# One transformer-like layer: gates closed in written order, squares one block later, and the last write of a triangular inverse moved with its transfers

## The chip, the cores and the metric

The kernel runs on one core of a Trainium2 chip. The metric is the device time of one execution in microseconds, the median of several runs. The engines of the core are TensorE (PE, matmuls), VectorE (DVE), ScalarE (ACT), GpSimd (POOL) and the DMA queues, some of them issued by SyncE (SP). Each engine runs its own list of instructions in the order in which the program holds them, and waits on semaphores for the others.

## What is computed

One layer of a hybrid decoder on 1024 tokens of width 1024, batch 1:

```python
h  = rms_norm(x)
P  = h @ W_in              # all heads and the gates
A  = rwkv7(P)              # 8 heads x 64, delta-rule state
B  = stick_breaking(P)     # 8 heads x 64, causal, QK-norm
M  = memory_attention(P)   # 4 heads x 128, 256 memory tokens, QK-norm
x += (sum_b sigmoid(G_b) * (branch_b @ W_br[b])) @ W_out
x += conv_ffn(rms_norm(x))
```

In stick-breaking attention a token's weight for an earlier token is a sigmoid times the product of one minus the sigmoids of all tokens between, a scan along the keys. The memory attention is a softmax over 256 tokens. The RWKV heads are computed in chunks of 64 tokens, and each chunk needs the inverse of a 64 x 64 triangular matrix.

## The kernel before, in words

Every product with weights runs in split precision: `split_w` (L77 to L91) loads a weight tile `wr` of 128 x 1024, ACT rounds it to `wh` (L80), POOL takes the rest `wl` (L81), and `mm3` gives PE three matmuls for one, all recorded at L115. `wh` and `wl` have two buffers each, so the L80 of the weights after next waits until PE has read the last of the present ones. A `proj_item` is one such product: 8 steps over the inner dimension, two PSUM banks `mm` as its result, and a `yield` after each step, so that it can be cut into pieces. A `gate_item` is a projection followed by an eviction (ACT, L820), a product with the norm (DVE, L821) and, as `close`, a sigmoid (ACT, L824) and a store to DRAM (`gsd`). Closes are collected in `open_gates` and run at step 4 of the next projection (`close_gates`).

The layer is written as a chain of main parts, each woven with a stream of such items (`weave`, `pumped`): after each yield of the main part a ratio says how many pieces of the stream follow. The main parts are the preparation of RWKV (up to about 325 us of the span), `sb_attn` (to about 620), `mem_attn` (with items that must come before it, to about 760), and `stage2`, the second half of RWKV; behind them come the branches, the output projection and the feed-forward part. A second filler, `inverse`, is advanced from `pumped` as well: `pace[0]` says how many tenths of a step per piece, 7 during `sb_attn` and 16 during `mem_attn`. It builds the triangular inverses in the tile `inst` with 62 pairs of DVE operations (L545 into a temporary `it`, one buffer, and L547 back into `inst`), writes the diagonal of ones (L549) and sends the result to DRAM in 16 transfers `td` (L554), issued by POOL. Stage 2 uses a tile `it` too, the next user of that one buffer, and clears it on POOL (L564).

A unit of `sb_attn` has a `front` (PE makes scores in one or two PSUM banks `g`; ACT's sigmoid L920 reads them out), `weigh` (the scan L926 on DVE), `mid` (PE transposes, L105, into banks `g`; ACT copies them out, L938) and `back` (PE; ACT L961 reads out). There are four banks `g` and four `mm`. The stream's items at this time are, for each of four pairs of heads p, the k projection, a gate, the q projection and another gate. Their `fin` functions evict with L842 and L871 and then square (L843, L872) for the norm of the heads: PE sums the squares in a bank `g`, DVE reads it (`head_norm`, L766 and L170), POOL finishes the scale (L171, then L770 or L772, tiles `hf` and `nf`). L863 to L866 split the keys and L881, L882 the queries into high and low parts.

A block of `mem_attn` has the same shape: PE makes scores in two banks `g`; DVE takes the maximum (L1137) and from it and the head's scale `hf` a bias `nb` (L1140); ACT runs the exponential (L1143) four times for a block, in place of the read-out; DVE normalises (L1147, L1149). Two blocks later PE transposes and ACT evicts (L1158), again two blocks later PE multiplies with the values, ACT evicts (L1168) and stores. There are 8 blocks, two for each head. The items woven with it are memory queries (`mem_q`, evictions L1105 to L1107) and gates.

What fixes the order: PE's matmuls are `pinned`, which keeps them in the order in which they are written; so are the inverse's two operations, the scan and L1105 and L1107. `ordered` does the same for one instruction anywhere. All other instructions of ACT, DVE, POOL and the queues are placed by the scheduler, which runs through the program with its own costs and takes what is ready by priority; what stands first in an engine's list can therefore change when anything near it changes.

## Time and profile before

| | us |
|---|---|
| median of 3 runs | 1806.98 (1806.52 to 1807.33) |
| the profiled execution | 1807.54 |
| its span, first to last instruction | 1805.8 |
| PE busy | 1779.9 |
| DVE / ACT / POOL busy | 1178.7 / 864.3 / 789.1 |
| granted TensorE clock | 0.999 |

In a line of the timeline stand: start, duration, engine, source line, operation, what it writes and reads with shapes, how many instructions the line gathers (x), and in brackets the idle time of the engine before it with what ended it. Matmuls overlap: a line of several matmuls is busy a little beyond the start of the next. Most lines are given with source lines of the kernel before; in the changed file everything below the inverse stands two or three lines later (L772 is L774 there, L920 is L923, L1158 is L1161).

### The profile page before, as it was taken

To read this page: it belongs to the slowest core of one execution; us is meant where nothing else is said; L and a number is where in the kernel's file an instruction comes from. 1 tells how busy PE (TensorE), PEld (TensorE's weight loads), DVE (VectorE), ACT (ScalarE), POOL (GpSimd) and SP (SyncE) were. 2 spreads that over 40 slices of the span, in tenths; PEclk is the share of its full clock that TensorE was granted. 3 is DMA by queue.
4 is the path that set the end of the run, shared out by engine and by line. 5 is a ranking of instruction groups with operands and counts; after the bars stand their busy time and mean duration, and the time that the engine had idled before them with its cause. 6 is when DMAs were issued, how large, how long until landed. Compare 5 with 4: busy or idle time off the path is not lost.

```text
span 1805.8 us, 27326 instructions
## 1 busy us (share of the span) xinstructions
PE 1779.9 (99%) x10479; PEld 1442.8 (80%) x10479; DVE 1178.7 (65%) x1625; ACT 864.3 (48%) x1556; POOL 789.1 (44%) x448
## 2 busy tenths in 40 slices
PE   9999999999999999999999999989999999999998
PEld 7777778888888888777777878868888888878877
DVE  5667775898987534244444872587767777794596
ACT  6444344566566535534444334544444444454343
POOL 3223353322231462122332541487677677545454
PEclk9999999999999999999999999999999999999999
DMA  5155564211112352567654552323323333395475
GB/s 208 59 163 176 196 209 156 73 42 45 53 56 88 113 131 78 191 241 267 216 187 176 185 199 106 105 88 113 109 88 107 109 111 111 119 341 191 137 261 181
DMA packets 122628, 261.29 MB, mean 145 GB/s; under 512 B 28665, under 2 KB 43385, under 8 KB 122370
## 3 DMA queue, kind: packets, MB, share of 16 engines
q1 hardware_dynamic: 84882, 193.70, 32.4%
q10 hardware_dynamic: 33840, 53.23, 8.0%
q0 software_dynamic: 3776, 12.62, 2.3%
q8 instruction: 82, 1.34, 0.3%
q14 instruction: 48, 0.39, 0.1%
HBM read 178.99 MB, written 80.48 MB: 144 GB/s over the span
## 4 chain that ended last, share of the span: by engine, by line
PE 66%; DVE 7%; issue 3%; DMA 3%; ACT 3%; POOL 2%; ACTq 0%; DVEq 0%; POOLq 0%; SPq 0%
PE mm L115 55%; PE g L115 8%; PE g L105 3%; DMA wr<-in_w_out_dram 1%; DVE at L926 1%; DVE it L545 1%; POOL wl L81 1%; DMA A<-yd 1%; DVE da L1735 1%; DVE at L1287 0%; DVE mg L1294 0%; DVE inst L547 0%; DMA dx<-x2d 0%; DMA out_dram<-dx 0%; ACT at L1143 0%
## 5 line engine op out<-in xcount | busy, mean ns | idle before, releaser
L81 POOL TENSOR_TENSOR wl<-wr,wh 128x1024 fp32r<-128x1024 f32 (+2 forms) x78 | 195.2, 2504 | 502.1 <-ACT wh L80 492.5
L115 PE MATMUL mm<-xhi,wh 128*128 128x512 f32 x784 | 259.9, 412 | 0.5 <-DVE w L322 0.4
L115 PE MATMUL mm<-xlo,wh 128*128 128x512 f32 x784 | 243.7, 392 | 0.3 <-DVE xlo L199 0.3
L115 PE MATMUL mm<-xhi,wl 128*128 128x512 f32 x784 | 242.5, 391 | 0.0
L115 PEld LDWEIGHTS mm<-xlo,wh 128*128 128x128 f32 x784 | 147.2, 188 | 34.0 <-DVE xlo L199 1.1
L115 PEld LDWEIGHTS mm<-xhi,wl 128*128 128x128 f32 x784 | 146.8, 188 | 33.0 <-POOL wl L81 0.7
L115 PEld LDWEIGHTS mm<-xhi,wh 128*128 128x128 f32 x784 | 136.6, 189 | 28.7 <-issue 6.1
L80 ACT ACTIVATE wh<-wr 128x1024 fp32r<-128x1024 f32 (+2 forms) x78 | 81.8, 1048 | 146.8 <-PE mm L115 94.5
L115 PE MATMUL mm<-dw,da 128*128 128x512 f32 x528 | 121.9, 390 | 1.5 <-DVE da L1735 1.3
L115 PE MATMUL mm<-BT,l 128*128 128x512 f32 x504 | 118.0, 389 | 1.6 <-POOL l L1465 1.6
L115 PEld LDWEIGHTS mm<-dw,da 128*128 128x128 f32 x528 | 98.7, 188 | 24.0 <-DVE da L1735 3.1
L1736 POOL TENSOR_TENSOR dw<-draw,dw 128x512 fp32r<-128x512 f32 x55 | 81.8, 1496 | 82.5 <-ACT dw L1734 82.5
L115 PEld LDWEIGHTS mm<-BT,l 128*128 128x128 f32 x504 | 94.5, 188 | 21.6 <-POOL l L1465 2.0
L926 DVE TENSOR_TENSOR_SCAN at<-at,nrt 128x128 f32<-128x128 f32 (+3 forms) x64 | 94.2, 1478 | 25.5 <-ACT at L920 25.3
L115 PE MATMUL mm<-BT,wh 128*128 128x512 f32 x352 | 108.8, 390 | 1.6 <-DVE BT L1375 0.9
L115 PE MATMUL mm<-B,wh 128*128 128x512 f32 x352 | 108.5, 389 | 0.0
L1735 DVE TENSOR_TENSOR da<-draw,da 128x512 fp32r<-128x512 f32 x77 | 65.7, 863 | 58.7 <-ACT da L1733 58.2
L115 PE MATMUL g<-dw,da 128*128 128x512 f32 x396 | 90.8, 390 | 2.1 <-POOL dw L1736 1.1
L1465 POOL TENSOR_TENSOR l<-it,l 128x1024 fp32r<-128x1024 f32 x21 | 50.8, 2417 | 92.2 <-ACT l L1462 92.2
L115 PEld LDWEIGHTS g<-dw,da 128*128 128x128 f32 x396 | 74.3, 188 | 18.2 <-POOL dw L1736 1.4
L821 DVE TENSOR_TENSOR w<-w,nrt 128x1024 f32<-128x1024 f32 x24 | 49.8, 2076 | 58.5 <-ACT w L820 47.6
L1733 ACT ACTIVATE da<-draw 128x512 fp32r<-128x512 f32 x77 | 48.3, 628 | 82.6 <-PE mm L115 38.7
(335 smaller groups left out, 3977.9 us busy)
## 6 DMA issues: line engine op xcount, KB each, us to landing
wr<-in_w_in_dram SPq DMA_DIRECT2D x48, 512.0 KB, 3.6
draw<-actd SPq DMA_DIRECT2D x77, 256.0 KB, 4.0
draw<-in_w_down_dram SPq DMA_DIRECT2D x55, 256.0 KB, 4.9
at<-scr SPq DMA_DIRECT2D x24, 512.0 KB, 5.9
wr<-in_w_up_dram SPq DMA_DIRECT2D x22, 512.0 KB, 3.5
actd<-gall ACTq DMA_DIRECT2D x44, 256.0 KB, 3.5
rw<-in_w_up_dram SPq DMA_DIRECT2D x20, 512.0 KB, 3.7
gsd<-w ACTq DMA_DIRECT2D x18, 512.0 KB, 2.8
```

The lines of the kernel that those rows point to most:

```text
L80: self.nc.scalar.activation(hi, raw, AF.Copy)
L81: self.nc.gpsimd.tensor_tensor(lo, raw, hi.bitcast(F32), ALU.subtract)
L105: self.pinned(self.nc.tensor.transpose(out, in_, self.ident[:n, :n]))
L115: self.pinned(self.nc.tensor.matmul(*a, **k))
L545: self.pinned(nc.vector.tensor_tensor(tv, X[:, 0:s, s : s + 1].to_broadcast([128, s, n]), X[:, s : s + 1, s + 1 : 64].to_broadcast([128, s ...
L821: nc.vector.tensor_tensor(g, g, self.nrb, ALU.mult)
L926: self.pinned(nc.vector.tensor_tensor_scan(sn[:, :W][:, ::-1], sn[:, :W][:, ::-1], self.nrt[:, 1152 - W :][:, ::-1], 1.0, ALU.mult, ALU.max))
L1465: nc.gpsimd.tensor_tensor(lo, src, hi.bitcast(F32), ALU.subtract)
L1733: self.pinned(nc.scalar.activation(A[:, 0], a, AF.Copy))
L1735: self.pinned(nc.vector.tensor_tensor(A[:, 1], a, A[:, 0].bitcast(F32), ALU.subtract))
L1736: nc.gpsimd.tensor_tensor(Wt[:, 1], w, Wt[:, 0].bitcast(F32), ALU.subtract)
```

## The change

Five edits. (1) The inverse pauses for 8 more steps before it writes the diagonal, and that write keeps its written place; the inverse's steps during `mem_attn` come at half the rate (8 in place of 16), which spreads its 16 transfers. (2) The sigmoid that closes a gate keeps its written order on ACT. (3) The k projection of the first attention closes gates at its step 6, all others at 4 as before. (4) The squares of k and q are taken out of the read-out functions and run as hooks of the gate behind each: k's at step 1, q's at step 0. (5) The low half of the memory queries (L1107) is no longer pinned.

```diff
--- before.py
+++ after.py
@@ -546,7 +546,9 @@
             yield
             self.pinned(nc.vector.tensor_tensor(X[:, 0:s, s + 1 : 64], X[:, 0:s, s + 1 : 64], tv, ALU.add))
             yield
-        nc.vector.memset(X.rearrange("p s t -> p (s t)")[:, 0 : 64 * 64 : 65], 1.0)
+        for _ in range(8):
+            yield
+        self.ordered(nc.vector.memset(X.rearrange("p s t -> p (s t)")[:, 0 : 64 * 64 : 65], 1.0))
         for p in range(4):
             for h2 in range(2):
                 for cc in range(2):
@@ -772,14 +774,14 @@
         nc.gpsimd.tensor_tensor(v3(f), v3(f), b3(self.rsc), ALU.mult)
         return f
 
-    def proj_item(self, src, fin, hook={}):
+    def proj_item(self, src, fin, hook={}, close=4):
         w = self.split_w(src)
         yield
         out = [self.ps("mm"), self.ps("mm")]
         for k in range(8):
             ks = slice(k * 128, (k + 1) * 128)
             self.mm3(out, [a[:, ks] for a in w], self.xin(k), k == 0, k == 7)
-            if k == 4:
+            if k == close:
                 self.close_gates()
             if k in hook:
                 hook[k]()
@@ -821,7 +823,7 @@
             nc.vector.tensor_tensor(g, g, self.nrb, ALU.mult)
 
             def close():
-                nc.scalar.activation(g, g, AF.Sigmoid, scale=-1.0)
+                self.ordered(nc.scalar.activation(g, g, AF.Sigmoid, scale=-1.0))
                 if keep is None:
                     nc.scalar.dma_start(self.gsd[b, d], g)
                 else:
@@ -840,7 +842,6 @@
             kr, sq = self.t4(), self.t4()
             for h in range(2):
                 nc.scalar.activation(kr[:, h * 512 : (h + 1) * 512], pp[h], AF.Copy)
-            nc.scalar.activation(sq, kr, AF.Square)
             st["k"] = sq, kr
 
         def k_ss():
@@ -869,8 +870,10 @@
             qr, sq = self.t4(), self.t4()
             for h in range(2):
                 nc.scalar.activation(qr[:, h * 512 : (h + 1) * 512], pp[h], AF.Copy)
-            nc.scalar.activation(sq, qr, AF.Square)
             st["q"] = sq, qr
+
+        def square(name):
+            nc.scalar.activation(*st[name], AF.Square)
 
         def q_split(i):
             qr = st["q"][1]
@@ -888,9 +891,9 @@
             st["f"] = self.head_norm(self.head_ss(st["q"][0]), 2, SBD, SBD ** -0.5, nf)
 
         w = self.I["w_in"]
-        hooks = {1: lambda: k_split(1), 3: q_ss, 4: lambda: q_split(0), 6: lambda: q_split(1)}
+        hooks = {0: lambda: square("q"), 1: lambda: k_split(1), 3: q_ss, 4: lambda: q_split(0), 6: lambda: q_split(1)}
         kq = {4: k_bc, 5: lambda: k_split(0)}
-        return self.proj_item(w[18 + p], k_fin), k_ss, self.proj_item(w[14 + p], q_fin, kq), hooks
+        return self.proj_item(w[18 + p], k_fin, close=6), k_ss, self.proj_item(w[14 + p], q_fin, kq), {1: lambda: square("k")}, hooks
 
     def sb_attn(self, qk, need):
         nc = self.nc
@@ -1104,7 +1107,7 @@
                 hs = slice(i * 512, (i + 1) * 512)
                 self.pinned(nc.scalar.activation(qhi[:, hs], pp[i], AF.Copy, scale=self.par("memq")))
                 nc.scalar.activation(sq[:, hs], pp[i], AF.Square)
-                self.pinned(nc.vector.scalar_tensor_tensor(qlo[:, hs], pp[i], self.par("memq"), qhi[:, hs].bitcast(F32), ALU.mult, ALU.subtract))
+                nc.vector.scalar_tensor_tensor(qlo[:, hs], pp[i], self.par("memq"), qhi[:, hs].bitcast(F32), ALU.mult, ALU.subtract)
             st.extend((sq, qhi, qlo))
 
         def ss():
@@ -1868,8 +1871,8 @@
         gate = lambda hook={}: self.gate_item(*gq.pop(0), hook)
         mark = lambda name: lambda: marks.add(name)
         for p in range(4):
-            kp, kss, qp, hooks = self.sb_qk(p, qk[p])
-            items += [*([self.differ] if p == 0 else []), kp, gate({6: self.spread_last} if p == 0 else {}), kss, qp, gate(hooks), mark(f"sb{p}")]
+            kp, kss, qp, early, hooks = self.sb_qk(p, qk[p])
+            items += [*([self.differ] if p == 0 else []), kp, gate({**early, 6: self.spread_last} if p == 0 else early), kss, qp, gate(hooks), mark(f"sb{p}")]
         prep, mss, mv, mk = self.mem_kv()
         mqi = [None] * 4
         for h in range(4):
@@ -1904,7 +1907,7 @@
         need("sb0")
         self.weave(self.sb_attn(qk, need), pump, 1.03, 0)
         need("kv")
-        pace[0] = 16
+        pace[0] = 8
         self.weave(self.mem_attn(mq, need), pump, 1.6, 0)
         need("mem")
         st2 = self.stage2()
```

PE's list is the same in both programs. Three places on the other engines show what moved.

The first is ACT in pair 3 of the first attention, around the square of q (`w4` written from `w4`). Before:

```order
L871 ACTIVATE w4_785_4564<-mm_762_4404 128x512
L871 ACTIVATE w4_785_4564<-mm_763_4405 128x512
L80 ACTIVATE wh_791_4580<-wr_790_4578 128x1024
L872 ACTIVATE w4_786_4565<-w4_785_4564 128x1024
L920 ACTIVATE at_787_4569<-g_788_4570,nf_669_3925 128x512
L920 ACTIVATE at_787_4569<-g_789_4574,nf_669_3925 128x128
L938 ACTIVATE at_796_4594<-g_797_4595 128x384
```

and after:

```order
L872 ACTIVATE w4_785_4564<-mm_762_4404 128x512
L872 ACTIVATE w4_785_4564<-mm_763_4405 128x512
L80 ACTIVATE wh_791_4579<-wr_790_4577 128x1024
L923 ACTIVATE at_787_4568<-g_788_4569,nf_669_3925 128x512
L923 ACTIVATE at_787_4568<-g_789_4573,nf_669_3925 128x128
L876 ACTIVATE w4_786_4565<-w4_785_4564 128x1024
L941 ACTIVATE at_796_4594<-g_797_4595 128x384
```

The square stands behind the two score read-outs of the next unit and no longer ahead of them.

The second is POOL at the end of the first attention, where the first transfer `td` of the inverse stood. Before:

```order
L81 TENSOR_TENSOR wl_953_5427<-wr_951_5424,wh_952_5426 128x1024
L81 TENSOR_TENSOR wl_963_5468<-wr_961_5465,wh_962_5467 128x1024
L554 DMA td_75<-inst_94 8x64x64
L81 TENSOR_TENSOR wl_971_5505<-wr_969_5502,wh_970_5504 128x1024
L81 TENSOR_TENSOR wl_980_5554<-wr_978_5551,wh_979_5553 128x1024
L554 DMA td_75<-inst_94 8x64x64
```

and after:

```order
L81 TENSOR_TENSOR wl_953_5427<-wr_951_5424,wh_952_5426 128x1024
L81 TENSOR_TENSOR wl_963_5468<-wr_961_5465,wh_962_5467 128x1024
L566 MEMSET it_1184_6759 128x512
L81 TENSOR_TENSOR wl_971_5505<-wr_969_5502,wh_970_5504 128x1024
L81 TENSOR_TENSOR wl_980_5554<-wr_978_5551,wh_979_5553 128x1024
L81 TENSOR_TENSOR wl_987_5622<-wr_985_5619,wh_986_5621 128x1024
```

In the place of the transfer there is now stage 2's clearing of its tile `it`; both transfers shown have gone further down.

The third is the memory attention at block 6 (`at_1131`; its scale is `hf_1129`) and block 7 (`at_1145`, scores in `g_1147` and `g_1150`); `wh_1155` and `wl_1156` are the weights of a later item. ACT before:

```order
L1143 ACTIVATE at_1131_6474,sm_1132_6475<-g_1133_6476,nb_1135_6485,hf_1129_6457 128x256 x2
L1143 ACTIVATE at_1131_6474,sm_1132_6475<-g_1136_6489,nb_1138_6498,hf_1129_6457 128x256 x2
L1168 ACTIVATE at_1103_6332<-mm_1140_6514 128x512
L1158 ACTIVATE at_1141_6519<-g_1142_6520 128x512
L1169 DMA yd_76<-at_1103_6332 128x512
L1158 ACTIVATE at_1141_6519<-g_1143_6526 128x512
L80 ACTIVATE wh_1155_6584<-wr_1154_6582 128x1024
L820 ACTIVATE w4_1144_6544<-mm_1112_6366 128x512
L820 ACTIVATE w4_1144_6544<-mm_1113_6367 128x512
L824 ACT_TABLE_LOAD
L824 ACTIVATE w4_1144_6544<-w4_1144_6544 128x1024
```

and after:

```order
L80 ACTIVATE wh_1155_6584<-wr_1154_6582 128x1024
L822 ACTIVATE w4_1144_6544<-mm_1112_6366 128x512
L822 ACTIVATE w4_1144_6544<-mm_1113_6367 128x512
L1146 ACTIVATE at_1131_6474,sm_1132_6475<-g_1133_6476,nb_1135_6485,hf_1129_6457 128x256
L1161 ACTIVATE at_1141_6519<-g_1142_6520 128x512
L1146 ACTIVATE at_1131_6474,sm_1132_6475<-g_1133_6476,nb_1135_6485,hf_1129_6457 128x256
L1161 ACTIVATE at_1141_6519<-g_1143_6526 128x512
L1146 ACTIVATE at_1131_6474,sm_1132_6475<-g_1136_6489,nb_1138_6498,hf_1129_6457 128x256 x2
L1146 ACTIVATE at_1145_6548,sm_1146_6549<-g_1147_6550,nb_1149_6559,hf_1129_6457 128x256 x2
L1146 ACTIVATE at_1145_6548,sm_1146_6549<-g_1150_6563,nb_1152_6572,hf_1129_6457 128x256 x2
L1171 ACTIVATE at_1124_6419<-mm_1159_6602 128x512
```

The L80 and the two gate evictions (w4_1144) stand ahead of block 6's exponentials, and the two evictions of `at_1141` among them; the sigmoid of the gate and the table loads have gone down. POOL there, before:

```order
L772 TENSOR_TENSOR hf_1088_6251<-hf_1088_6251,rsc_351 128x8
L81 TENSOR_TENSOR wl_1111_6363<-wr_1109_6360,wh_1110_6362 128x1024
L171 TENSOR_TENSOR hf_1129_6457<-rs_1130_6458,half_340 128x8
L772 TENSOR_TENSOR hf_1129_6457<-hf_1129_6457,rsc_351 128x8
L81 TENSOR_TENSOR wl_1156_6585<-wr_1154_6582,wh_1155_6584 128x1024
```

and after:

```order
L81 TENSOR_TENSOR wl_1111_6363<-wr_1109_6360,wh_1110_6362 128x1024
L556 DMA td_75<-inst_94 8x64x64 x4
L171 TENSOR_TENSOR hf_1129_6457<-rs_1130_6458,half_340 128x8
L81 TENSOR_TENSOR wl_1156_6585<-wr_1154_6582,wh_1155_6584 128x1024
L774 TENSOR_TENSOR hf_1129_6457<-hf_1129_6457,rsc_351 128x8
```

The second step of the scale `hf_1129` now stands behind the `wl` of the weights. On DVE in the same way the gate's product L821 stands ahead of the two `nb` of block 6, and behind those of block 6 before.

## The prediction

> **What bounds the kernel now.** The page comes first, for the engines' shares.

> ```profile
> PE 1779.9 (99%) x10479; PEld 1442.8 (80%) x10479; DVE 1178.7 (65%) x1625; ACT 864.3 (48%) x1556; POOL 789.1 (44%) x448
> ```

> TensorE (PE) is busy for 99% of the span, and the change neither adds nor removes a matmul, nor moves one: PE's program is the same row for row before and after. So the time can only change where PE waits. The second view is PE's waits, cut to 300 to 800 us, the stretch that holds both attentions and all code that the change touches. Its columns are the waiting line, what it waited for, us in total, times, longest.

> ```profile
> PE mm L115 <- POOL wl L81: 2.3, 1, 2.3
> PE g L115 <- ACT at L920: 2.1, 3, 1.0
> PE g L115 <- DVE hn L766: 0.9, 1, 0.9
> PE g L105 <- DVE hn L766: 0.4, 1, 0.4
> PE g L105 <- ACT at L938: 0.2, 1, 0.2
> PE g L105 <- DVE w L335: 0.2, 1, 0.2
> ```

> That is 6.1 us in eight waits: the ceiling for a gain is 0.34% of the time, and there is no ceiling for a loss. The third view is the timeline of each engine around each of these waits, and around the places where the change puts something new in front of an instruction that PE needs.

> **First attention, the gain at 384 us.** First VectorE (DVE), then PE.

> ```profile
> 383.75 1.28 DVE L882 SCALAR_TENSOR_TENSOR qk<-w,params,qk 64x1024 fp32r<-64x1024 f32 x1
> 385.06 0.17 DVE L766 TENSOR_TENSOR hn<-g,rsc 128x16 f32<-128x16 f32 x1
> 386.36 2.04 DVE L926 TENSOR_TENSOR_SCAN at<-at,nrt 128x896 f32<-128x896 f32 x1
> 385.29 0.73 PE L115 MATMUL g<-qk,qk 128*128 128x512 f32 x2 [0.88 <-DVE hn L766]
> ```

> PE waits for L766 to read a PSUM bank, and L766 stands behind the query split L882. In the changed program this L766 comes ahead of that L882, so it can run at 383.75: 1.3 us sooner, and the wait of 0.88 goes. I book 0.9. It is kept if nothing on DVE stops PE next: L882 is then the late one, and the program order of DVE is the old one again from the scan at 386.36 on. Bounds 0 and 1.3.

> **First attention, the squares.** In pairs 2 and 3 the square of q (L872) now follows the two L920 of the next unit. ScalarE (ACT) and PE at pair 2, then DVE and PE of pair 3:

> ```profile
> 450.01 1.04 ACT L872 ACTIVATE w<-w 128x1024 f32<-128x1024 f32 x1
> 450.95 0.93 ACT L920 ACTIVATE at<-g,nf 128x512 f32<-128x512 f32 x2
> 451.68 0.51 PE L115 MATMUL g<-qk,qk 128*128 128x256 f32 x2 [1.01 <-ACT at L920]
> ...
> 536.46 0.17 DVE L766 TENSOR_TENSOR hn<-g,rsc 128x16 f32<-128x16 f32 x1
> 536.68 0.33 PE L105 MATMUL g<-kon,at 128*128 128x128 f32 x1 [0.37 <-DVE hn L766]
> ```

> L920 moves up by the square's 0.94 (450.95 less 450.01), and PE's wait of 1.01 shrinks to nearly nothing. The same happens at 525 in pair 3. But is it kept? The next row is DVE's share of the two stretches that follow:

> ```profile
> 434.00:481.30 47.30, 46.12 (x343) 38.20 (x342) 46.83 (x41) 27.19 (x49) 10.66 (x4) 1.00 0.12 41
> 517.80:539.60 21.80, 20.48 (x140) 16.29 (x140) 21.40 (x18) 16.07 (x32) 5.34 (x2) 1.00 0.21 61
> ```

> The third figure after the length is DVE: 46.83 of 47.30 us, and 21.40 of 21.80. DVE is full there, its order there is unchanged, and it ends each stretch with an L766 for which PE already waits (536.46, wait 0.37). PE arrives 0.94 sooner and waits 0.94 longer. I book 0 for both, upper bound 2 x 0.94 = 1.9.

> **First attention, the gates.** One gate's sigmoid stands ahead of an eviction L938:

> ```profile
> 582.55 1.07 ACT L824 ACTIVATE w<-w 128x1024 f32<-128x1024 f32 x1 [2.48 <-DVE w L821]
> 583.53 0.95 ACT L938 ACTIVATE at<-g 128x512 f32<-128x512 f32 x2
> 584.15 0.66 PE L105 MATMUL g<-kon,at 128*128 128x128 f32 x4 [0.23 <-ACT at L938]
> ```

> After, that sigmoid and its store come after the L938, so the 0.2 goes. Nobody in this stage reads a closed gate: it is stored to DRAM, and the later store costs nothing as long as its place among evictions leaves PE its banks. An eviction queued behind a late sigmoid would be 1.07 late; I see none there for which PE is due within that. Booked: 0.2.

> **The inverse.** GpSimd (POOL), then PE:

> ```profile
> 620.34 0.91 POOL L554 DMA_DIRECT2D td<-inst  x1 [3.02 <-DVE inst L547]
> 623.69 0.58 PE L115 MATMUL mm<-qk,wl 128*128 128x256 f32 x1 [2.28 <-POOL wl L81]
> 676.44 0.52 POOL L564 MEMSET it<- 128x512 f32 x1
> ```

> The first of 16 transfers waits 3.02 us for the inverse's last write, and the weight half wl queued behind it on POOL is what PE waits for, 2.28. It looks as if moving the transfers removes that wait. The new order says no: in the transfer's place stands the MEMSET of stage 2's tile `it` (second order piece above), which needs the very buffer that the inverse's last step reads; so it waits for the same L547. Only the body differs, 0.91 against 0.52. Booked: 0.4; bounds 0 and 2.3 (if the inverse ended sooner). The 16 transfers themselves (0.91 of POOL each) lie later in the memory attention, eight of them in a row (7.3 us) before a wl that PE needs only after another whole item: 0.

> **Memory attention, the small loss at 710 us.** ACT's L80 of the next weights now stands ahead of the exponentials of block 4. PE, then ACT:

> ```profile
> 708.48 0.63 PE L115 MATMUL mm<-xlo,wh 128*128 128x512 f32 x2
> 710.77 1.48 PE L115 MATMUL g<-A,qk 128*128 128x256 f32 x11
> 705.39 0.56 ACT L1143 ACTIVATE at<-g,nb,hf 128x256 f32<-128x256 f32 x1
> 711.48 1.08 ACT L80 ACTIVATE wh<-wr 128x1024 fp32r<-128x1024 f32 x1
> ```

> L80 overwrites weights that PE reads until 708.48 + 0.63 = 709.1, so it cannot start sooner, and ends at 710.2. Two exponentials behind it, 0.56 each, end at 711.3; they free the bank in which PE starts block 5 at 710.77. Loss: 711.35 - 710.77 = 0.6, bounds 0 and 1.1.

> **Memory attention, the large loss at 730 us.** The same at block 6, with more in the chain (third order piece). The rows of before, ACT, POOL, DVE, PE:

> ```profile
> 724.07 0.57 ACT L1143 ACTIVATE at<-g,nb,hf 128x256 f32<-128x256 f32 x1 [5.17 <-DVE nb L1140]
> 727.33 0.60 ACT L1158 ACTIVATE at<-g 128x512 f32<-128x512 f32 x1
> 729.50 1.06 ACT L80 ACTIVATE wh<-wr 128x1024 fp32r<-128x1024 f32 x1 [1.58 <-PE mm L115]
> ...
> 720.98 0.20 POOL L772 TENSOR_TENSOR hf<-hf,rsc 128x8 f32<-128x8 f32 x1
> 730.64 2.40 POOL L81 TENSOR_TENSOR wl<-wr,wh 128x1024 fp32r<-128x1024 f32 x1 [9.46 <-PE g L115]
> ...
> 723.83 0.28 DVE L1140 SCALAR_TENSOR_TENSOR nb<-mxt,hf 128x2 f32<-128x2 f32 x2
> 732.00 2.12 DVE L821 TENSOR_TENSOR w<-w,nrt 128x1024 f32<-128x1024 f32 x1
> 734.04 0.22 DVE L1140 SCALAR_TENSOR_TENSOR nb<-mxt,hf 128x2 f32<-128x2 f32 x2
> ...
> 729.76 1.48 PE L115 MATMUL g<-A,qk 128*128 128x256 f32 x11
> ```

> Before, the scale hf of this head is final at 721.2, the exponentials of block 6 run from 724.07, two evictions L1158 follow, the last from 727.33, and PE starts block 7 at 729.76 without waiting. After, three orders chain up. (1) On POOL L772, which finishes hf, stands behind wl; wl needs wh, whose L80 must wait until PE has done with the old weights, 729.50. So wl runs 730.64 to 733.04 and L772 ends at 733.3. (2) On DVE the gate's L821 now stands ahead of the nb of block 6. In before it started at 732.00 beside POOL's wl and ended at 734.12, 1.08 after wl did; I take 734.1 again, since the wl is the same. (3) On ACT the exponentials stand behind L80 and the two L820, and behind the first exponential stands the L1158 whose bank PE takes for block 7. From nb at 734.04 the first exponential starts 0.24 later (723.83 to 724.07), 734.3; the L1158 some 0.6 later, 734.9; it ends at 735.5. PE starts block 7 at 735.55 and not at 729.76: loss 5.8.

> [...]

> ```profile
> 396.11 1.22 DVE L821 TENSOR_TENSOR w<-w,nrt 128x1024 f32<-128x1024 f32 x1
> ```

> [...] The upper end is 8.0: if the bank were one that the last of block 6's four exponentials frees, 4 x 0.56 = 2.2 further on. PE reads block 6's weights only two blocks later, so nothing more is late.

> Two table loads fewer stand in this stage, since the sigmoid comes after all exponentials now:

> ```profile
> 735.22 1.28 ACT L1143 ACT_TABLE_LOAD   x1
> 736.51 0.56 ACT L1143 ACTIVATE at<-g,nb,hf 128x256 f32<-128x256 f32 x1
> ```

> 2 x 1.28 of ACT, where PE does not wait: 0. [...]

> **The sum.** Gains 0.9 + 0 + 0.2 + 0.4 = 1.5; losses 0.6 + 5.8 = 6.4; net +4.9. The profiled execution took 1807.54 us (span 1805.8), 0.56 above the median of the runs, 1806.98. It would take 1812.4; the median 1806.98 + 4.9 = **1811.9**.

> **The rivals.** What this kernel's times can tell from no change is about 0.2%, 3.6 us: faster is below 1803.4, slower above 1810.6.

> A, the forecast, 57%: both losses come as worked out; gains from 0.4 to 3.5 and losses from 5.7 to 6.9 give +2.2 to +6.5, 1809.2 to 1813.5. Two thirds of it lie above 1810.6.

> B, the other side, 26%: the wait at block 7 does not come. Its place is the bank: 4 banks of this kind take turns, and if PE is handed one that was emptied at 727.33 or before, the late exponentials have two blocks of time until PE reads them. For it: nothing in the trace shows which bank the new program waits for. Against it: the new order has all bank releases after 729.5 behind the chain. It decides from the point at which the L1158 ahead of block 7 ends before 729.8. Then only the gains are left, with 0 to 0.6 lost: 1.5 booked gives 1805.5 to 1806.1 (10%), and with the squares' 1.9 and the whole 2.3 at 621 kept, 1806.98 - 0.9 - 1.9 - 0.2 - 2.3 = 1801.7 (16% for 1801.7 to 1803.4).

> C, 17%: PE gets the last bank (8.0), and DVE takes back the gain at 384 as it does the squares': 0.6 + 8.0 - 0.2 = +8.4, 1815.4; more where a late sigmoid adds a wait of its 1.07.

> That the change does nothing is no case of its own: with all terms off by half it falls into A's lower or B's upper part.

> Above 1810.6: two thirds of A and all of C, 38% + 17% = 0.55. Below 1803.4: 0.16. Between: 0.29. The range leaves out most of B's fast part and what lies above C: 1803.4 to 1815.4. A's own is 1809.2 to 1813.5.

> **What would show it.** In the profile after: among PE's waits one new row of 5 to 6 us for the eviction L1158 (L1161 after) or the exponential, near 730; POOL's L772 after a wl; the wait on DVE L766 of 0.88 gone; POOL wl at 1.9 in place of 2.3; the L920 waits down by 2 us and those on L766 up by as much. If PE's wait near 730 is absent the forecast is wrong by its largest term.

## The result, and the profile after

| | before | after |
|---|---|---|
| median, us (7 runs each) | 1807.29 | 1812.50 |
| the profiled execution | 1807.54 | 1811.39 |
| its span | 1805.8 | 1809.6 |

The ratio is 1.0027 with a 95% interval of 1.0017 to 1.0036: slower by 0.27%, 4.9 us of 1807.29. The forecast was 4.9 more.

PE's waits after, from 300 to 810 us (the columns are those of the prediction; source lines are two or three higher):

```profile
PE g L115 <- ACT at L1161: 5.6, 1, 5.6
PE g L105 <- DVE hn L768: 2.1, 2, 1.3
PE mm L115 <- POOL wl L81: 1.6, 1, 1.6
PE g L115 <- ACT at L1146: 0.4, 1, 0.4
PE mm L115 <- DVE qk L1110: 0.3, 1, 0.3
```

The one wait of 5.6 stands where none was. The waits on the read-out L920 (2.1) have gone from the head of the list; in their place L768 (L766 before) has two, 2.1 in all, and the 0.9 at 384 is not among them.

Block 7 of the memory attention after, ACT, POOL, DVE and PE in turn, all about 2.0 us sooner on the clock than in before, since that much had been gained by then:

```profile
727.46 1.06 ACT L80 ACTIVATE wh<-wr 128x1024 fp32r<-128x1024 f32 x1 [2.58 <-PE mm L115]
732.31 0.56 ACT L1146 ACTIVATE at<-g,nb,hf 128x256 f32<-128x256 f32 x1 [2.82 <-DVE nb L1143]
732.87 0.59 ACT L1161 ACTIVATE at<-g 128x512 f32<-128x512 f32 x1
...
728.60 2.34 POOL L81 TENSOR_TENSOR wl<-wr,wh 128x1024 fp32r<-128x1024 f32 x1 [9.66 <-ACT wh L80]
730.90 1.18 POOL L774 TENSOR_TENSOR hf<-hf,rsc 128x8 f32<-128x8 f32 x1
...
729.52 2.50 DVE L823 TENSOR_TENSOR w<-w,nrt 128x1024 f32<-128x1024 f32 x1 [7.65 <-ACT w L822]
732.11 0.23 DVE L1143 SCALAR_TENSOR_TENSOR nb<-mxt,hf 128x2 f32<-128x2 f32 x2
...
733.50 2.93 PE L115 MATMUL g<-A,qk 128*128 128x256 f32 x12 [5.63 <-ACT at L1161]
736.23 1.05 PE L115 MATMUL mm<-xhi,wh 128*128 128x512 f32 x2
737.81 0.62 PE L115 MATMUL mm<-xhi,wl 128*128 128x512 f32 x2
```

The chain is the one that was worked out, instruction for instruction: L80, wl, the gate's product, nb, the first exponential, the eviction, PE. None of its steps waits for a transfer. Only the scale L774 ends later than forecast, with the product and not ahead of it, which costs nothing here: nb stands behind the product on DVE anyway. The last three lines show what was not worked out. The twelve matmuls of block 7 take 2.93 and not the 1.5 to 1.6 of the blocks elsewhere, and two of the next step 1.05, before they are at 0.62 again: PE runs at half its rate after the wait. The windows show it as the granted clock (the figure after POOL's), first before at 623.69, behind its wait of 2.28, then after at the same place behind 1.59, and after behind 5.63:

```profile
623.69:627.50 3.81, 3.81 (x19) 3.81 (x20) 0.00 (x0) 0.00 (x0) 3.03 (x2) 0.56 0.56 165
```

```profile
622.00:626.00 4.00, 3.92 (x42) 3.79 (x44) 0.00 (x0) 0.25 (x1) 2.38 (x2) 1.00 0.49 147
733.50:736.50 3.00, 3.00 (x13) 3.00 (x14) 1.31 (x5) 2.42 (x8) 0.00 (x0) 0.50 0.36 131
```

Since PE's list is the same, the start of every matmul can be set against its start in before. The steps in that difference are the account of the change:

| place, us of before | what changes | us |
|---|---|---|
| 384 | wait on L766 gone | -1.1 |
| 450, then 460 | wait on L920 gone, wait on L766 new | -1.0, +0.9 |
| 525, then 536 | the same | -0.9, +1.0 |
| 584 and 602 to 607 | sigmoid out of the way; small shifts | -0.3 |
| 621 | wait 2.28 to 1.59 | -0.7 |
| 624 to 627 | half rate behind the wait gone | -1.5 |
| 693 to 698 | small shifts | -0.1 |
| 711 and 714 | block 5: waits on L1146 and L1110 | +1.2 |
| 730 | wait before block 7 | +5.8 |
| 730 to 732 | half rate behind it | +1.9 |
| sum to 760 | | +5.2 |
| 1047 | a wait on DVE's L1286 that differs from profile to profile | -1.6 |

PE of the changed kernel is 0.4 late already at 300 us in this pair of profiles, ahead of all that is counted here, and 3.8 late at the end of the span.

### The profile page after: what moved, and what is told of

The parts are those of the page before. It is cut to its first block, busy times and chain, and to the rows that moved or that the text cites. A ratio compares the mean times of both kernels' runs of the same rounds, so it can differ in the third digit from the quotient of the medians.

```text
span 1809.6 us, 27344 instructions
## 1 busy us (share of the span) xinstructions
PE 1781.1 (98%) x10479; PEld 1442.9 (80%) x10479; DVE 1175.1 (65%) x1625; ACT 863.1 (48%) x1554; POOL 790.8 (44%) x448
## 4 chain that ended last, share of the span: by engine, by line
PE 47%; DVE 4%; DMA 4%; issue 2%; POOL 2%; ACT 1%; SPq 0%; DVEq 0%; POOLq 0%; ACTq 0%
PE mm L115 40%; PE g L115 6%; DMA draw<-actd 1%; PE g L105 1%; DMA draw<-in_w_down_dram 1%; DMA wr<-in_w_out_dram 1%; DMA A<-yd 0%; DVE at L1290 0%; DVE mg L1297 0%; DVE da L1738 0%; DVE at L1289 0%; POOL dw L1739 0%; DMA out_dram<-it 0%; DVE it L1758 0%; DMA mrd<-w 0%
## 5 line engine op out<-in xcount | busy, mean ns | idle before, releaser
L81 POOL TENSOR_TENSOR wl<-wr,wh 128x1024 fp32r<-128x1024 f32 (+2 forms) x78 | 197.2, 2529 | 506.4 <-ACT wh L80 503.8
L115 PE MATMUL mm<-xhi,wh 128*128 128x512 f32 x784 | 260.7, 413 | 0.5 <-DVE w L322 0.4
L115 PE MATMUL mm<-xlo,wh 128*128 128x512 f32 x784 | 243.9, 392 | 0.0
L115 PE MATMUL mm<-xhi,wl 128*128 128x512 f32 x784 | 242.5, 391 | 0.2 <-POOL wl L81 0.2
L115 PEld LDWEIGHTS mm<-xlo,wh 128*128 128x128 f32 x784 | 147.4, 188 | 33.5 <-DVE xlo L199 0.4
L115 PEld LDWEIGHTS mm<-xhi,wl 128*128 128x128 f32 x784 | 147.1, 188 | 33.5 <-POOL wl L81 1.0
L115 PEld LDWEIGHTS mm<-xhi,wh 128*128 128x128 f32 x784 | 137.0, 190 | 29.1 <-issue 6.1
L80 ACT ACTIVATE wh<-wr 128x1024 fp32r<-128x1024 f32 (+2 forms) x78 | 81.7, 1048 | 148.3 <-PE mm L115 88.0
L115 PE MATMUL mm<-dw,da 128*128 128x512 f32 x528 | 121.8, 390 | 1.2 <-DVE da L1738 0.9
L115 PE MATMUL mm<-BT,l 128*128 128x512 f32 x504 | 117.9, 389 | 1.6 <-POOL l L1468 1.6
L115 PEld LDWEIGHTS mm<-dw,da 128*128 128x128 f32 x528 | 98.7, 188 | 23.6 <-DVE da L1738 2.7
L929 DVE TENSOR_TENSOR_SCAN at<-at,nrt 128x128 f32<-128x128 f32 (+3 forms) x64 | 98.4, 1546 | 26.1 <-ACT at L923 25.8
L115 PEld LDWEIGHTS mm<-BT,l 128*128 128x128 f32 x504 | 94.5, 188 | 21.6 <-POOL l L1468 2.0
L115 PE MATMUL mm<-BT,wh 128*128 128x512 f32 x352 | 108.8, 390 | 1.6 <-DVE BT L1378 0.9
L115 PE MATMUL mm<-B,wh 128*128 128x512 f32 x352 | 108.4, 389 | 0.0
L115 PE MATMUL g<-dw,da 128*128 128x512 f32 x396 | 90.8, 390 | 2.1 <-POOL dw L1739 1.1
L115 PEld LDWEIGHTS g<-dw,da 128*128 128x128 f32 x396 | 74.2, 188 | 18.2 <-ACT dw L1737 1.5
```

The costliest lines, as they stand in the source:

```text
L80: self.nc.scalar.activation(hi, raw, AF.Copy)
L81: self.nc.gpsimd.tensor_tensor(lo, raw, hi.bitcast(F32), ALU.subtract)
L115: self.pinned(self.nc.tensor.matmul(*a, **k))
L929: self.pinned(nc.vector.tensor_tensor_scan(sn[:, :W][:, ::-1], sn[:, :W][:, ::-1], self.nrt[:, 1152 - W :][:, ::-1], 1.0, ALU.mult, ALU.max))
```

## The experiments

The theory after the result: the loss is the order of block 6 and its half-rate tail, the edit behind that order is the rate of the inverse's steps, and the squares bring nothing because DVE's L766 takes it back. The rivals are named in each expectation. Line numbers in the experiments' rows shift by a few lines with the edits. "Before" was run again on the same chip each time; all ratios are to it.

**The rate taken back.**

```diff
-        pace[0] = 8
+        pace[0] = 16
```

> The changed kernel with one number taken back: the inverse's steps during the memory attention at 16 again in place of 8. With 16 the program has block 4's and block 6's exponentials ahead of the L80 of the weights again, and the scale hf ahead of wl on POOL; the rest stays changed. Theory: the loss is this order alone, with two parts in the trace after, the waits of PE (5.6 before block 7, 0.4 and 0.3 at block 5) and the half TensorE rate for the microseconds behind the long wait, 1.9. All of it goes: after minus 8.5, about 3.5 us under the kernel before, ratio to it 0.998. No wait on L1161 (L1158) near 730; 621 waits 1.6 as after. Rival 1, the spread transfers themselves cost the time (DMA queue, POOL): then the transfers at 16 bring back nothing of the wait at block 7. Rival 2, the half rate is only a matter of the records: after minus 6.4, 1.5 under before.

Measured: 1805.24 against 1807.84, ratio 0.9984 (0.9975 to 0.9992). All of PE's waits of 300 to 810:

```profile
PE g L105 <- DVE hn L768: 2.2, 2, 1.4
PE mm L115 <- POOL wl L81: 1.6, 1, 1.6
PE g L105 <- DVE w L335: 0.2, 1, 0.2
PE g L115 <- ACT at L923: 0.2, 1, 0.2
```

No wait on ACT or DVE in the memory attention is left. With one number the changed kernel goes from 0.27% slower to 0.16% faster, 0.43% or 7.8 us, of 8.9 counted in the table (blocks 5 and 7). This run takes the transfers' spread back together with the order, so by itself it can't tell the two apart. For the order speak the chain above, in which nothing waits for a transfer, and the next run, which has the same rate with another order and waits 8.2 before block 7 and not 5.6. The old order at the new rate was not tried.

**The inverse's edit alone.** The kernel before with the eight pauses, the `ordered` write and the rate 8.

> The kernel before with the inverse's edit alone: 8 pauses, the diagonal's write in its written place, rate 8. Its program has the bad order of block 6 and, since the sigmoid is free, even the gate's sigmoid with two table loads ahead of block 6's first exponential. Theory: PE waits before block 7 for 5.6 plus sigmoid 1.06 plus table load 1.28 and some tenths, about 8.2, half rate behind it 1.9, block 5 0.7 to 1.0; the wait at 621 falls from 2.3 to 1.6 to 1.9, and the half rate behind it (1.5 in before) goes: net 8.2 + 1.9 + 1.0 - 2.1 = +9.0, ratio 1.005. Rival, the loss needs the gates' order: no wait over 2 us before block 7, ratio 0.999.

Measured: 1821.03 against 1807.84, ratio 1.0073 (1.0060 to 1.0086): more than expected.

```profile
PE g L115 <- ACT at L1160: 8.2, 1, 8.2
PE mm L115 <- DVE qk L1109: 3.2, 1, 3.2
```

The wait before block 7 is the 8.2 that the added sigmoid and table load give. The miss is the second line. At block 5 the low half of the memory query (L1107, L1109 here) is still pinned, stands on DVE behind an `nb` and a normalisation that wait for the late exponentials, and holds a bank that PE needs; the half rate follows it (granted clock 0.52 from 715.2 to 718.5 us, four matmuls in 3.54 where the four at 703.00 take 1.88). In the changed kernel the fifth edit has unpinned it, and its wait is 0.3.

**The same, with L1107 unpinned.**

```diff
-                self.pinned(nc.vector.scalar_tensor_tensor(qlo[:, hs], pp[i], ...))
+                nc.vector.scalar_tensor_tensor(qlo[:, hs], pp[i], ...)
```

> The kernel of e2_inverse_alone with the low half of the memory queries unpinned, too, as the change has it. In its program the first L1107 (L1109 here) stands ahead of the nb that waits for block 5's exponentials, and no longer behind it. Theory: the wait of 3.2 at block 5 goes but for 0.3, and the half rate behind it (1.5): 4.4 less than e2_inverse_alone, ratio to before 1.0049; the 8.2 before block 7 stays. Rival, block 5 is late for another reason: ratio 1.007 as there.

Measured: 1818.53 against 1807.58, ratio 1.0057 (1.0044 to 1.0070); in the profile PE is 4.4 ahead of the former at the end. Block 5 gives 4.5 (2.9 of wait, 1.6 of rate); 0.9 of it is given back by 900 us, most of it behind block 7, and 1.2 come near the end (it was 0.3 ahead before block 5). So the fifth edit takes away most of what the inverse's edit costs at block 5. The intervals of the two ratios overlap, so how much of it the median keeps is not shown, and what the edit does by itself was not tried.

**The squares alone.** The kernel before with L843 and L872 as hooks.

> The kernel before with the squares' edit alone, read-outs and hooks. Theory: the two waits of 1.0 on the read-out L920 (450 and 525 us) go and come back as waits on DVE's L766 10 us later (0.9 at 460, 1.3 at 536), since DVE is full between: net 0, ratio 1.000 within 0.0004. Rival, DVE has slack and the gain is kept: minus 1.9, ratio 0.999.

Measured: 1807.74 against 1807.84, ratio 0.9998 (0.9989 to 1.0007).

```profile
PE mm L115 <- POOL wl L81: 2.3, 1, 2.3
PE g L105 <- DVE hn L766: 2.2, 2, 1.4
PE g L115 <- DVE hn L766: 0.9, 1, 0.9
```

The 2.1 on L920 has become 2.2 on L766. Matmul for matmul: -0.94 at 451.68, +0.93 at 460.71, -0.90 at 527.12, +0.99 at 536.68. The interval alone would not exclude half of the 1.9; the four steps do.

**The sigmoid's order alone.** The kernel before with L824 `ordered`.

> The kernel before with the gates' sigmoid kept in its written place, alone. In its program the L766 of pair 1 is ahead of L882 on DVE, so this edit is the source of the gain at 384. Theory: minus 1.1 at 384 and minus 0.4 at 584: minus 1.5, ratio 0.9992; the waits on L766 0.9 and on L938 0.2 are gone, no wait over 1 us at 730. Rival, the later sigmoids cost ACT as much elsewhere: 1.000, with a new wait in 330 to 620.

Measured: 1805.53 against 1807.84, ratio 0.9990 (0.9981 to 0.9999). The `g L115` wait on L766 and the one on L938 are gone; PE gains 1.1 at 384 and 0.4 at 584. This edit is where the first attention's gain comes from. Every step of the table between 384 and 607 us stands in this profile or in that of the squares, so nothing there is left for the third edit (the close at step 6), which was not tried alone.

**The clearing of `it` moved off POOL**, on top of the first experiment.

```diff
-        nc.gpsimd.memset(ut, 0.0)
+        nc.vector.memset(ut, 0.0)
```

> The kernel of e1_pace16 with stage 2's clearing of its tile it moved from POOL to DVE, so that on POOL nothing waits for the inverse ahead of the wl that PE needs at 621. Theory: the wait of 1.6 at 621 goes, nothing takes its place on DVE, which only queues the clearing behind its own last inverse step: e1 minus 1.6, about 5 us under before, ratio 0.997. Rival, wl is late anyway because its wh is (ACT) or because DVE and POOL lock each other out: 1.0 or more of the wait stays.

Measured: 1802.84 against 1808.17, ratio 0.9975 (0.9965 to 0.9986). POOL around the former wait:

```profile
613.49 2.40 POOL L81 TENSOR_TENSOR wl<-wr,wh 128x1024 fp32r<-128x1024 f32 x1 [4.08 <-ACT wh L80]
616.37 2.47 POOL L81 TENSOR_TENSOR wl<-wr,wh 128x1024 fp32r<-128x1024 f32 x1 [0.48 <-ACT wh L80]
```

The second wl no longer waits for the inverse, and no wait on wl is left. The price is on DVE: an inverse step of 0.35 lasts until wl has gone,

```profile
616.63 2.42 DVE L545 TENSOR_TENSOR it<-inst 128x180 f32<-128x180 f32 x1
```

and nobody waits for it there.

**q's sums of squares one step earlier**, on top of that.

```diff
-        hooks = {0: lambda: square("q"), 1: lambda: k_split(1), 3: q_ss, ...}
+        hooks = {0: lambda: square("q"), 1: lambda: k_split(1), 2: q_ss, ...}
```

> The kernel of e5_dve_clear with q's sums of squares one step earlier, at step 2 of the gate in place of 3, on PE and so for DVE's L766. In its program L766 stands one row higher in pair 2 (ahead of an inverse step of 1.1) and two rows higher in pair 3 (1.9). Theory: what takes the squares' gain back is L766's place; higher by 1.1 and 1.9 it lets PE keep 0.9 at 460 and 1.0 to 1.35 at 536: minus 1.9 to minus 2.2 against e5, about 7 under before, ratio 0.996. Rival, PE then waits for the scan behind it, since DVE is full: within 0.5 of e5.

Measured: 1801.00 against 1808.17, ratio 0.9963 (0.9951 to 0.9976). DVE in pair 3:

```profile
531.46 1.76 DVE L929 TENSOR_TENSOR_SCAN at<-at,nrt 128x768 f32<-128x768 f32 x1
533.14 0.15 DVE L768 TENSOR_TENSOR hn<-g,rsc 128x16 f32<-128x16 f32 x1
533.41 0.97 DVE L545 TENSOR_TENSOR it<-inst 128x782 f32<-128x782 f32 x1
```

L768 stands ahead of the inverse's two steps, and both waits on it are gone: 0.4 us is all that PE still waits between 300 and 810. This version is faster than both kernels, 0.37% under before.

**What binds at block 7: the scale on POOL, or the gate's product on DVE?** The changed kernel with the second step of the scale on DVE.

```diff
-        nc.gpsimd.tensor_tensor(v3(f), v3(f), b3(self.rsc), ALU.mult)
+        (nc.vector if nh == 1 else nc.gpsimd).tensor_tensor(v3(f), v3(f), b3(self.rsc), ALU.mult)
```

> The changed kernel with the second step of the memory queries' scale hf (L772, L774 after) on DVE in place of POOL, so that no scale waits behind wl. ACT's and DVE's bad order of block 6 stays in its program (L80 and the gate's L821 ahead of block 6's nb and exponentials); block 4's order is the good one again. Theory: the gate's product on DVE, which POOL's wl holds off until it has ended, binds as much as the scale: the wait before block 7 stays between 5.0 and 5.8, and only block 5's 1.0 goes: ratio to before 1.002. Rival, the scale on POOL is what binds: the wait falls by 1 or more, to under 4.6.

Measured: 1814.68 against 1808.17, ratio 1.0037 (1.0024 to 1.0050).

```profile
728.08 2.34 POOL L81 TENSOR_TENSOR wl<-wr,wh 128x1024 fp32r<-128x1024 f32 x1 [9.56 <-ACT wh L80]
...
728.95 2.55 DVE L823 TENSOR_TENSOR w<-w,nrt 128x1024 f32<-128x1024 f32 x1 [7.65 <-ACT w L822]
731.42 0.15 DVE L774 TENSOR_TENSOR hf<-hf,rsc 128x8 f32<-128x8 f32 x1
```

```profile
PE g L115 <- ACT at L1161: 5.8, 1, 5.8
```

POOL's wl, DVE's product and scale, and below them PE's wait: it is 5.8 with no scale behind wl: the gate's product alone, held off by wl and then 1.1 long, binds as tightly. The rival falls. The expected gain at block 5 came (no wait there), but a wait of 0.7 on L1146 near 695 and 2.3 lost behind block 7, where the changed kernel lost 1.9, took it back; the rest of the difference to 1.002 lies behind 1030 us.

**The wait filled with matmuls.** The changed kernel with

```diff
+            if v == 7:
+                d = self.ps("mm")
+                for _ in range(22):
+                    self.mmul(d, self.kx[0][:, 0:128], self.kx[0][:, 0:512], start=True, stop=True)
```

at the head of the block's `front`; nothing is left out, the product is not read.

> The changed kernel with 22 extra matmuls of 128x512 (22 x 0.227 = 5.0 us) into an unused bank ahead of block 7, in the place where PE waits 5.6; their result is not read. All other instructions stand in the same order. Theory: the 5.6 us of wait are filled but for some tenths, PE does not go to half rate behind it, and block 7 and the step behind it take 1.5 and 0.45 again: minus 1.9 against after, ratio to before 1.0017 where after has 1.0027; by span 1.9 less than after. Rival, block 7 is slow because its operands or the DMA are (the extra work changes nothing): same as after, or a little longer.

> The changed kernel once more, beside its filled-up twin on one chip. Theory: ratio 1.0027, the waits of the first profile (5.6 before block 7, 1.6 at 621, 0.4 and 0.3 at block 5) again; what differs between profiles of one kernel is the wait on DVE's L1289 in 1030 to 1050 us, 0.6 in the first.

> The changed kernel with the 22 extra matmuls ahead of block 7 once more, beside the changed kernel itself. Theory: PE is 1.9 ahead of it behind block 7, as in the first profile, and the median is 1 to 2 us lower than that of the changed kernel on the same chip; the first run's equal medians came from the later stretch, where profiles differ by up to 1.5. Rival: medians equal again within 0.5, so that what the full rate brings at block 7 is really given back later.

Measured: filled 1812.56 against 1808.17, ratio 1.0029 (1.0020 to 1.0037); the second time, on one chip, the changed kernel 1813.19 (1.0029, 1.0019 to 1.0040) and the filled one 1814.23 (1.0031, 1.0020 to 1.0043), before 1807.58. PE in the first filled run:

```profile
727.63 5.15 PE L115 MATMUL mm<-A 128*128 128x512 f32 x22
733.49 1.70 PE L115 MATMUL g<-A,qk 128*128 128x256 f32 x12 [0.71 <-ACT at L1165]
735.02 0.63 PE L115 MATMUL mm<-xhi,wh 128*128 128x512 f32 x2
```

The mechanism is shown: PE starts block 7 at the same time, 733.5, but at full rate (granted clock 1.00 from 733 to 740 us), and is 1.9 ahead of the changed kernel from 738 on, in both pairs of profiles. The expected time did not come: by 1060 us most of it is gone. In the second filled run PE waits 1.9 on DVE's L1293 (L1286 before) near 1050 where the changed kernel beside it waited 0.5, and falls to half rate there (two matmuls take 1.06 from 1052.45 on, and 0.62 from 1055.59). The waits on that line add up to between 0.6 and 2.5 us in the thirteen profiles of this study, without a clear relation to how early PE came (0.6 and 1.2 in the two profiles of the changed kernel itself); whether the filled kernel is unlucky twice or pays there for being earlier stays open. So the 1.9 of half rate is a loss at its place, and its part in the median is not shown.

## Why the prediction was right, point by point

- **PE's waits as the ceiling, and the order as what decides.** The order is right. The ceiling is too low: with the same matmuls the difference is a sum of waits and of the rate behind them, and the 6.1 us of waits leave out the 1.5 that PE loses at half rate behind 621. The last version of the experiment on the sums of squares is 7.7 us ahead of before between 300 and 800 us, more than the ceiling, and 0.37% faster by the runs, where the ceiling was 0.34%.
- **384 us:** 0.9 booked, 1.1 measured, and kept. The source is the sigmoid's order (its experiment alone), which the prediction did not say.
- **Squares:** 0 booked against 1.9 by the waits' own rows, because L766 behind a full DVE was next. Measured 0.0 net in the changed kernel, ratio 0.9998 alone. The experiment on the sums of squares shows the same from the other side: with L766 higher the 1.9 is there.
- **Gates:** 0.2 booked, 0.3 measured.
- **621 us:** 0.4 booked for the wait, 0.7 measured: in the transfer's place the MEMSET waits for the same L547, as argued. Of the 0.7, 0.4 is the shorter body; the rest is that the MEMSET starts 0.06 us after that last write, where the transfer started 0.31 after it. But 1.5 more was gained, since the half rate behind the wait went. This row was mis-sized at 0.4 and came to 2.2, and the sign of it was in the profile of before, in the granted clock of 0.56.
- **Block 5:** 0.6 booked with 1.1 as the upper end; measured 0.7 where PE waits on L1146, as worked out, and 0.6 where it waits on the unpinned L1110, which the prediction did not have: 1.2 in all.
- **Block 7:** 5.8 booked, 5.8 measured. PE was handed the bank of the first eviction, as forecast; rival B (another bank) and C (the last bank, 8.0) did not happen. The lower end of A's losses, 5.7, counts 5.1 here, for a gate's product that ends ahead of hf; no run shows that term: in after and in the run with the scale on DVE the product ends 1.08 after the wl beside it and is 2.50 and 2.55 long, where the L821 at 396.11 of before, with no wl beside it, takes 1.22. The half rate, 1.9, was not booked.
- **The sum:** +4.9 forecast, +4.9 by the ratio, +5.2 counted up to 760 us; the two profiled executions are 3.8 apart, as 1.6 came back at 1047. The agreement is closer than the terms deserve: the two unbooked half-rate terms, -1.5 and +1.9, nearly cancel, and so do the extra 0.6 lost at block 5 and the extra 0.6 gained at 384, the gates and the wait at 621.

## What to carry to other kernels

A change of a filler's rate or of a few priorities cost or brought here what it did to the order on the other engines; list those orders, and price each place where something PE needs has slipped behind something that waits for PE. When a wait goes, look at once for who is late next, on a full engine at the next instruction that frees a bank: unless that one moves too, the gain can go back, as it did twice here. And count behind a long wait what the half rate costs there: 1.5 behind 2.28 us, 1.9 behind 5.63 here. In one profile two waits that stand close together, 0.98 and 1.10, had such a tail as well.

## What the runs showed of the hardware

Half rate after a pause. Behind waits of 2.28 (before), 3.15 (the inverse's edit alone) and 5.63 us (after) PE ran for 3.4 to 4.1 us at half its rate (granted clock 0.56, 0.52 and 0.50 in windows there), a loss of 1.5 to 1.9 each; behind 1.59 it stayed at 1.00. At 1.8 us the length of a wait did not decide it. In the second run of the changed kernel a wait of 1.79 had a tail (the windows show the stretch of the wait, PE busy for 1.61, and the two behind it):

```profile
1194.63 5.74 PE L115 MATMUL mm<-BT,l 128*128 128x512 f32 x17 [1.79 <-POOL l L1468]
```

```profile
1191.68:1195.08 3.40, 1.61 (x8) 1.03 (x7) 1.33 (x2) 3.40 (x6) 3.40 (x3) 1.00 0.44 141
1195.10:1198.50 3.40, 3.40 (x10) 2.61 (x9) 3.40 (x7) 2.42 (x5) 3.32 (x3) 0.50 0.23 35
1198.52:1201.90 3.38, 3.38 (x16) 2.78 (x16) 2.53 (x4) 0.62 (x2) 3.38 (x3) 1.00 0.32 130
```

A wait of 1.80 in the run of the inverse's edit alone had none:

```profile
1203.08 4.15 PE L115 MATMUL mm<-BT,l 128*128 128x512 f32 x17 [1.80 <-POOL l L1467]
```

```profile
1199.62:1203.03 3.41, 1.66 (x8) 1.04 (x6) 0.83 (x2) 3.41 (x5) 3.41 (x3) 1.00 0.36 86
1203.08:1206.48 3.40, 3.40 (x15) 2.82 (x16) 3.39 (x6) 2.42 (x5) 3.40 (x2) 1.00 0.29 74
```

Two waits of about one microsecond had a tail in the second run of the changed kernel, and the same two had none in its first profile. The second run, then the first, each with the window behind the waits as its third line:

```profile
1756.83 0.50 PE L115 MATMUL g<-dw,da 128*128 128x512 f32 x1 [0.98 <-ACT dw L1737]
1758.44 4.77 PE L115 MATMUL g<-dw,da 128*128 128x512 f32 x13 [1.10 <-POOL dw L1739]
1758.30:1761.70 3.40, 3.26 (x8) 2.59 (x9) 3.40 (x4) 0.83 (x2) 2.05 (x3) 0.50 0.52 167
```

```profile
1754.17 0.50 PE L115 MATMUL g<-dw,da 128*128 128x512 f32 x1 [1.03 <-ACT dw L1737]
1755.79 4.38 PE L115 MATMUL g<-dw,da 128*128 128x512 f32 x18 [1.11 <-POOL dw L1739]
1755.79:1759.20 3.41, 3.41 (x15) 2.83 (x16) 3.39 (x4) 0.69 (x2) 2.06 (x2) 1.00 0.67 175
```

| | PE idle in the piece, % | the next piece |
|---|---|---|
| before, from 620.22 | 64.8 | half rate |
| after, from 727.39 | 85.6 | half rate |
| after, from 730.80, itself at half rate | 79.2 | half rate |
| all others of both, at most | 46.9 | full rate |

The two cases of 1.8 us lie between: by the windows above PE was idle for 52.6% of the one ahead of the tail and for 51.3% of the one without. Full rate came back behind a piece in which PE worked for 3.35 of 3.41 us (before) and for all of it (after). What between 51.3 and 52.6% makes the difference is not shown. The two profiles of the changed kernel are 3.3 us apart, and the first of the two tails above, which only one of them has, is about 1.6 of it: PE is 1.10 later than in the first profile ahead of that tail (1194.63 against 1193.53) and 2.66 later at 1756.83 (against 1754.17).

DVE and POOL in each other's way. The gate's product took 2.50 beside wl, where the L821 at 396.11 of before took 1.22 with no wl beside it, and the short scale step on POOL then 1.18 in place of 0.20, until the product had ended; moved off POOL, the clearing let wl hold up an inverse step for 2.42 in place of 0.35. Such a pair cost 1.3 and 2.1 here, beside a wl of 2.3 to 2.5. At block 7 both instructions wait on ACT, so ACT's order sets which of the two is first.
